# Gate and up as 2x2 block products, with seven products for three of eight pairs of k tiles

## The chip, the cores and the metric

One NeuronCore of a Trainium2 chip runs the whole program. The metric is device time in microseconds, lower is better: 2230.7 us is the median of three runs of the kernel before (2228.87 to 2231.47).

## What is computed

The reference is an encoder of two layers on 256 tokens of width 2048, all in float32. Layer 0 mixes tokens by neighbourhood attention and a gated recurrence, layer 1 by pooling and grouped-query attention. After each mixer every layer does the same:

```
x = layer_norm(ALPHA * x + mixer(x), g1, b1)
f = (silu(x @ w_gate) * (x @ w_up)) @ w_down      # 2048 -> 5632 -> 2048
x = layer_norm(ALPHA * x + f, g2, b2)
```

## The kernel before

All matrix products are made from float32 values that are split in two: `hi`, the value rounded to the matmul's format (fp32r), and `lo`, the remainder. One product of a 128x128 tile of x with a 128x512 tile of weights is three matmuls of 512 columns into one PSUM bank (`mm3`, line 243): x lo by w hi, x hi by w hi, x hi by w lo. x lies transposed in `xT`, as hi and lo, 16 k tiles for each of the two token tiles (`tok`) of 128.

Weights come from HBM in halves: `load_half` (line 140 issues the load on SyncE's queue) brings 128 x 1024 elements, 512 KB, which are two k tiles by 512 columns, into one of four `raw` buffers. ScalarE rounds them into `whi` (line 103) and VectorE subtracts to make `wlo` (line 104). `whi` and `wlo` rotate through a ring of slots, and a slot is rounded into again when TensorE has used it up. Each half feeds 12 matmuls.

The feed-forward part, `ffn`, walks 11 chunks of 512 hidden columns in three phases (`PHASES`: 3, 4 and 4 chunks). A chunk is 8 halves of gate into two banks, Silu on ScalarE (line 367), 8 halves of up into two more, the product of the two on VectorE (line 374), four transposes for each token tile (line 100, TensorE with the identity) and the split into `yT`. After the chunks of a phase come the products with w_down (`in_down`), four column blocks of 512, whose results are added to the residual `res` (lines 257 and 259). At the last block of the last phase the halves are all loaded first and the tokens go one after the other (`tok_major`), so that the layer norm of token tile 0 runs beside the products of tile 1. `out_proj`, which stands ahead of `ffn`, is built in the same way. PSUM's eight banks are three for `acc`, two for `tr` (transposes) and three for `mx`.

The order of instructions on each engine is made when the program is built: a scheduler runs a model of the engines and takes what is ready by priority, which `tc.high_priority` raises. On the chip each engine follows its own fixed order, and semaphores hold an instruction until its inputs are there. So an engine that waits holds up all that stands behind it in its order.

Of the kernel before, what the change touches and what calls it, by code (L numbers as in the profile page):

```python
# [11 lines left out]
F32 = mybir.dt.float32  # L12
F32R = mybir.dt.float32r
# [5 lines left out]
P = 128  # L19
# [4 lines left out]
NCH = 512  # L24
# [45 lines left out]


@with_exitstack
def trunk(ctx: ExitStack, tc: tile.TileContext, a, out):
# [7 lines left out]
    ps = ctx.enter_context(tc.tile_pool(name="ps", bufs=1, space=PSUM))  # L81
# [8 lines left out]
    def acc():  # L90
        return ps.tile([P, NCH], F32, tag="acc", name="acc", bufs=3)

    def trp():
        return ps.tile([P, NCH], F32, tag="tr", name="tr", bufs=2)

    def mxp():
        return ps.tile([P, NCH], F32, tag="mx", name="mx", bufs=3)
# [12 lines left out]
    rings = [(wp, 6)]  # L110
# [38 lines left out]

    def mm_chunk(halves, lhs, outs, tok_major=False, after=None, before=None):  # L150
# [8 lines left out]
        def mms(i, tok, pin=False):  # L159
            hi, lo = loaded[i]  # L160
            k0 = halves[i][1]
            for kk in range(2):
                xh, xl = lhs(tok, k0 + kk)
# [171 lines left out]
    def out_proj(w, order, groups, res, gb):  # L335
        evac, norm = residual_tools(res, *gb)
        lhs = y_lhs(groups)
        xT = new_xT()
        for n in range(4):
            outs = [acc() for _ in range(NT)]  # L340
            halves = [(w[n, 2 * g + i], 4 * g + 2 * i) for g in order for i in range(2)]
# [11 lines left out]
    def ffn(fp, layer, xT, res, gb, last):  # L353
        evac, norm = residual_tools(res, *gb)
        lhs = x_lhs(xT)
        new = None if last else new_xT
        nxt = [None]
        for pi, chunks in enumerate(PHASES):
            groups = {}
            for c in chunks:  # L360
                first = pi == 0 and c == 0
                gouts = [acc() for _ in range(NT)]
                sil = {}

                def silu(tok):
                    sil[tok] = fp.tile([P, NCH], F32, tag="sil", name="sil", bufs=3)
                    nc.scalar.activation(sil[tok], gouts[tok], AF.Silu)

                mm_chunk([(a[f"gate{layer}"][c, i], 2 * i) for i in range(8)], lhs, gouts, tok_major=first, after=silu)
                uouts = [acc() for _ in range(NT)]  # L370
                groups[c] = new_yT()

                def gated(tok):
                    nc.vector.tensor_tensor(sil[tok], sil[tok], uouts[tok], op=mult)
                    s = slice(tok * P, (tok + 1) * P)
                    transpose4(sil[tok], groups[c][0][:, :, s], groups[c][1][:, :, s])

                mm_chunk([(a[f"up{layer}"][c, i], 2 * i) for i in range(8)], lhs, uouts, after=gated)
            end = pi == len(PHASES) - 1
            if end and not last:  # L380
                nxt[0] = new_xT()
            gl = [groups[c] for c in chunks]
            for n in range(4):
                outs = [acc() for _ in range(NT)]
                halves = [(a[f"down{layer}"][n, 2 * c + i], 4 * ci + 2 * i) for ci, c in enumerate(chunks) for i in range(2)]

                def after(tok):
                    with tc.high_priority(offset=1000 if end and n == 3 else 0):
                        evac(tok, n, outs[tok], pi == 0, end)
                        if end and n == 3:  # L390
                            norm(tok, nxt[0], out if last else None)

                mm_chunk(halves, y_lhs(gl), outs, tok_major=(end and n == 3), after=after)
        return nxt[0]
# [29 lines left out]
    def ab_mixer(mp, xT, yT):  # L424
# [239 lines left out]
        for c, ((kind, i), _) in enumerate(ab_plan()):  # L664
            outs = [acc() for _ in range(NT)]
            mm_chunk([(a["ab_in"][c, n], 2 * n) for n in range(8)], lhs, outs, before=load_x if c == 0 else None)
# [5 lines left out]
    def cd_mixer(mp, xT, yT):  # L672
# [118 lines left out]
        for c, (kind, _) in enumerate(cd_plan()):  # L791
            outs = [acc() for _ in range(NT)]
            mm_chunk([(a["cd_in"][c, n], 2 * n) for n in range(8)], lhs, outs, tok_major=(c == 0))
# [10 lines left out]
    with tc.tile_pool(name="ab", bufs=1) as mp:  # L804
        ab_mixer(mp, xT, yT)
# [4 lines left out]
    open_ring(ctx.enter_context(tc.tile_pool(name="wx", bufs=1)), 2)  # L810
    with tc.tile_pool(name="f0", bufs=1) as fp:
        open_ring(fp, 3)
        xT = out_proj(a["ab_out"], AB_OUT_GROUPS, yT, res, load_gb(fp, 0, "mix"))
        xT = ffn(fp, 0, xT, res, load_gb(fp, 0, "ffn"), False)
    rings.pop()
    yT = [new_yT() for _ in range(4)]
    with tc.tile_pool(name="cd", bufs=1) as mp:
        cd_mixer(mp, xT, yT)
    with tc.tile_pool(name="f1", bufs=1) as fp:
        open_ring(fp, 3)  # L820
        xT = out_proj(a["cd_out"], CD_OUT_GROUPS, yT, res, load_gb(fp, 1, "mix"))
        ffn(fp, 1, xT, res, load_gb(fp, 1, "ffn"), True)
# [54 lines left out]

def layout(i):
# [26 lines left out]
    for l in range(2):  # L905
        m[f"gate{l}"] = pieces(f["ffn_w_gate"][l])
        m[f"up{l}"] = pieces(f["ffn_w_up"][l])
# [24 lines left out]
```

## Time and profile before

| | |
|---|---|
| median of 3 runs | 2230.7 us |
| profiled execution | 2229.76 us |
| its span, first to last instruction | 2228.0 us |
| TensorE busy | 2201.6 us, 10180 instructions |
| VectorE busy | 1313.6 us, 1662 instructions |
| ScalarE busy | 994.5 us, 1258 instructions |
| loads | 416.78 MB from HBM, 188 GB/s over the span |
| granted TensorE clock | 0.996 of full speed |

Times are microseconds. PE is TensorE, DVE VectorE, ACT ScalarE, SP SyncE. A matmul's busy time overlaps the next one's, so the distance between starts tells its cost, not its duration. A row of a group gives the number of instructions, their busy time and the mean in ns; what follows is the idle time before them and what ended it.

### The profile page before, as it was taken

How to read it: one execution, taken by the hardware profiler on the slowest of the kernel's cores; microseconds unless marked ns; L12 is line 12 of the kernel's file. 1: busy time of each engine (PE TensorE's matmuls, PEld its weight loads, DVE VectorE, ACT ScalarE, POOL GpSimd, SP SyncE). 2: the span in 40 equal slices, each digit the busy share in tenths (PEclk: the TensorE clock that was granted, in tenths of full speed). 3: DMA queues.
4: the chain of work that ended last, by engine and by line, in shares of the span. 5: the costliest groups of instructions: out<-in, count | busy, mean ns of one | idle time of the engine just before them, and what ended most of it. 6: DMA issues, size and time to landing. Idle time of an engine off the chain costs nothing.

```text
span 2228.0 us, 26810 instructions
## 1 busy us (share of the span) xinstructions
PE 2201.6 (99%) x10180; PEld 1833.9 (82%) x10180; DVE 1313.6 (59%) x1662; ACT 994.5 (45%) x1258; POOL 83.1 (4%) x67
## 2 busy tenths in 40 slices
PE   8999999999999999999999999999999999999997
PEld 7888888887888888888888788878888888888886
DVE  6886688667555545554455676665554554544454
ACT  6445544546443444344443564444444444444431
POOL 0010001002000000000000200020000000000001
PEclk9999999999999999999999999999999999999999
DMA  8555545676655556565656464656555555656562
GB/s 293 161 161 180 173 130 183 219 250 211 205 187 191 190 188 194 184 199 184 197 176 199 151 207 141 235 171 227 188 190 192 186 192 186 198 179 201 183 197 71
DMA packets 118898, 420.66 MB, mean 189 GB/s; under 512 B 14448, under 2 KB 17008, under 8 KB 117488
## 3 DMA queue, kind: packets, MB, share of 16 engines
q1 hardware_dynamic: 118768, 418.94, 57.4%
q8 instruction: 80, 1.31, 0.2%
q14 instruction: 50, 0.41, 0.1%
HBM read 416.78 MB, written 2.10 MB: 188 GB/s over the span
## 4 chain that ended last, share of the span: by engine, by line
PE 96%; DVE 2%; ACT 1%; DMA 0%; issue 0%; POOL 0%; DVEq 0%; ACTq 0%; POOLq 0%
PE acc L243 91%; PE tr L100 2%; PE mx L530 1%; PE mx L243 1%; DVE wlo L104 1%; DVE xTl L319 0%; PE mx L576 0%; PE mx L783 0%; ACT whi L103 0%; ACT res L288 0%; DVE res L274 0%; DMA raw<-in_cd_in 0%; DMA x<-in_xT 0%; DVE res L278 0%; PE mx L766 0%
## 5 line engine op out<-in xcount | busy, mean ns | idle before, releaser
L104 DVE TENSOR_TENSOR wlo<-raw,whi 128x1024 fp32r<-128x1024 f32 (+1 forms) x761 | 938.4, 1236 | 726.2 <-ACT whi L103 708.8
L103 ACT CAST whi<-raw 128x1024 fp32r<-128x1024 f32 (+1 forms) x761 | 800.6, 1053 | 987.4 <-PE acc L243 836.2
L243 PE MATMUL acc<-whi,xTl 128*128 128x512 f32 x2080 | 814.7, 394 | 13.7 <-DVE xTl L319 8.0
L243 PE MATMUL acc<-whi,xTh 128*128 128x512 f32 x2080 | 814.4, 392 | 0.0
L243 PE MATMUL acc<-wlo,xTh 128*128 128x512 f32 x2080 | 808.7, 391 | 0.3 <-DVE wlo L104 0.3
L243 PEld LDWEIGHTS acc<-whi,xTl 128*128 128x128 f32 x2080 | 392.3, 189 | 93.5 <-DVE xTl L319 8.5
L243 PEld LDWEIGHTS acc<-wlo,xTh 128*128 128x128 f32 x2080 | 392.0, 188 | 81.6 <-DVE wlo L104 0.7
L243 PEld LDWEIGHTS acc<-whi,xTh 128*128 128x128 f32 x2080 | 392.4, 189 | 78.5
L243 PE MATMUL acc<-whi,yTl 128*128 128x512 f32 x960 | 375.0, 391 | 0.1
L243 PE MATMUL acc<-whi,yTh 128*128 128x512 f32 x960 | 373.8, 389 | 0.0
L243 PE MATMUL acc<-wlo,yTh 128*128 128x512 f32 x960 | 370.0, 389 | 0.0
L243 PEld LDWEIGHTS acc<-wlo,yTh 128*128 128x128 f32 x960 | 180.2, 188 | 37.8 <-DVE wlo L104 0.4
L243 PEld LDWEIGHTS acc<-whi,yTl 128*128 128x128 f32 x960 | 180.3, 188 | 37.0 <-DVE yTl L789 0.3
L243 PEld LDWEIGHTS acc<-whi,yTh 128*128 128x128 f32 x960 | 180.3, 188 | 36.7
L200 POOL TENSOR_TENSOR rstd<-rstd,mhalf 128x4 f32<-128x4 f32 (+2 forms) x18 | 17.6, 976 | 1799.8 <-DVE rstd L197 1656.9
L104 DVE TENSOR_TENSOR yTl<-tr,yTh 128x512 fp32r<-128x512 f32 x48 | 31.1, 686 | 79.5 <-ACT yTh L103 79.5
L103 ACT CAST yTh<-tr 128x512 fp32r<-128x512 f32 x48 | 26.0, 589 | 94.4 <-PE tr L100 94.3
L320 POOL TENSOR_TENSOR res<-res,bet 128x512 f32<-128x512 f32 x24 | 39.4, 1650 | 26.0 <-PE tr L100 14.6
L259 DVE TENSOR_TENSOR res<-res,acc 128x512 f32<-128x512 f32 x32 | 21.9, 685 | 25.4 <-PE acc L243 24.9
L530 PEld LDWEIGHTS mx<-qq,kk 128*128 128x128 f32 x256 | 33.6, 191 | 2.6
L530 PE MATMUL mx<-qq,kk 128*128 128x128 f32 x256 | 33.8, 274 | 0.0
L257 DVE SCALAR_TENSOR_TENSOR res<-res,acc 128x512 f32<-128x512 f32 x32 | 21.8, 683 | 16.7 <-PE acc L243 15.7
(162 smaller groups left out, 829.4 us busy)
## 6 DMA issues: line engine op xcount, KB each, us to landing
raw<-in_gate SPq DMA_DIRECT2D x176, 512.0 KB, 3.9
raw<-in_up SPq DMA_DIRECT2D x176, 512.0 KB, 4.3
raw<-in_down SPq DMA_DIRECT2D x176, 512.0 KB, 4.1
raw<-in_ab_in SPq DMA_DIRECT2D x127, 512.0 KB, 4.1
raw<-in_cd_in SPq DMA_DIRECT2D x40, 512.0 KB, 4.3
raw<-in_ab_out SPq DMA_DIRECT2D x32, 512.0 KB, 4.7
raw<-in_cd_out SPq DMA_DIRECT2D x32, 512.0 KB, 4.0
x<-in_xT SPq DMA_DIRECT2D x8, 256.0 KB, 6.3
```

What stands on the lines that cost most here:

```text
L100: return nc.tensor.transpose(o, src, eye)
L103: nc.scalar.copy(hi, src)
L104: nc.vector.tensor_tensor(lo, src, hi.bitcast(F32), op=sub)
L200: nc.gpsimd.tensor_tensor(r[:, :n], r[:, :n], mhalf[:, :n], op=ALU.pow)
L243: ins = nc.tensor.matmul(o, lhs[a], rhs[b], start=start and n == 0, stop=stop and n == 2)
L257: nc.vector.scalar_tensor_tensor(r, r, ALPHA, psum, op0=mult, op1=add)
L259: nc.vector.tensor_tensor(r, r, psum, op=add)
L320: nc.gpsimd.tensor_tensor(r, r, bet[:, s], op=add)
L530: nc.tensor.matmul(m[:, 2 * h + s, :], kk[:, h, s * P : (s + 1) * P], qq[:, h, r * P : (r + 1) * P], start=True, stop=True,)
```

## The change

A pair of k tiles (k1, k2) with the two token tiles, and gate and up as two columns, is a 2x2 by 2x2 block product: eight products of 128x128 by 128x512. `unit` does a chunk as eight pairs in the order of `PAIRS`. Five pairs are plain: their eight products go to four banks, c11 and c21 (gate of token tile 1 and 2), c12 and c22 (up). The pairs in `SEVEN` (5, 6 and 7) take seven products in the manner of Strassen and Winograd: three with weights as they are, four with sums of weights. `load_seven` loads the four blocks of a pair at once, 1 MB into the single buffer `rs`, makes four sums `z` on VectorE and splits the three plain blocks and the four sums into `sh` and `sl` (two buffers each). `forms_of` makes, once per layer, the four sums of x blocks for the three pairs (`fs`, split into `fm`); its buffer `xs` has the tag of `rs`, and `fs` that of `z`. Four of the seven products have banks of their own (p1, p6, p5, p7), which `unit` combines with c11 to c22 at the end of a chunk.

A unit so takes all eight banks: `open_banks("sides")` lays PSUM out as two sides of four, a unit's c banks on one and its p banks on the other, and the sides swap. Chunk 0 stays as it was (`whole`), as do the down products. The ring of weight slots is 4 during units (6 to 11 before), with 7 more around out_proj and around the last phase's down product. Gate and up lie together in HBM as `gu`, with up's two k tiles swapped. The diff, cut:

```diff
@@ -68,6 +68,9 @@
+PAIRS = (0, 1, 5, 2, 3, 6, 4, 7)
+SEVEN = (5, 6, 7)
...
@@ -78,7 +81,23 @@
-    ps = ctx.enter_context(tc.tile_pool(name="ps", bufs=1, space=PSUM))
+    banks = {}
+    def open_banks(kind):
+        if banks:
+            banks["stack"].close()
+        stack = ctx.enter_context(ExitStack())
+        pool = stack.enter_context(tc.tile_pool(name="ps", bufs=1, space=PSUM, reuse_waits="tile"))
+        banks.update(stack=stack, pool=pool, kind=kind, side=0)
+    def bank(tag, bufs):
+        return banks["pool"].tile([P, NCH], F32, tag=tag, name=tag, bufs=bufs)
+    def side_bank(other=False):
+        return bank("ab"[banks["side"] ^ other] + "side", 4)
...
@@ -88,13 +107,13 @@
     def acc():
-        return ps.tile([P, NCH], F32, tag="acc", name="acc", bufs=3)
+        return bank("acc", 3) if banks["kind"] == "uses" else side_bank()
     def trp():
-        return ps.tile([P, NCH], F32, tag="tr", name="tr", bufs=2)
+        return bank("tr", 2) if banks["kind"] == "uses" else side_bank(True)
...
@@ -107,7 +126,7 @@
-    rings = [(wp, 6)]
...
@@ -350,48 +371,160 @@
+    def forms_of(sp, xT):
+        n = len(SEVEN)
+        k = [slice(2 * SEVEN[0] + e, 2 * SEVEN[0] + 2 * n, 2) for e in range(2)]
+        xs = sp.tile([P, NT, 2 * n, P], F32, tag="rs", name="xs", bufs=1)
+        for t in range(NT):
+            s = slice(2 * SEVEN[0], 2 * SEVEN[0] + 2 * n)
+            nc.vector.tensor_tensor(xs[:, t], xT[0][t][:, s, :].bitcast(F32), xT[1][t][:, s, :].bitcast(F32), op=add)
+        x11, x12, x21, x22 = (xs[:, t, e : 2 * n : 2, :] for t in range(2) for e in range(2))
+        fs = sp.tile([P, 4, n, P], F32, tag="z", name="fs", bufs=1)
+        e, f, g, h = (fs[:, i] for i in range(4))
+        nc.vector.tensor_tensor(e, x22, x21, op=sub)
+        nc.vector.tensor_tensor(f, e, x11, op=add)
+        nc.vector.tensor_tensor(g, x11, x21, op=sub)
+        nc.vector.tensor_tensor(h, x12, f, op=sub)
+        hi, lo = split_tile(sp, [P, 4, n, P], fs, "fm")
+        out = []
+        for i in range(n):
+            k1, k2 = 2 * SEVEN[i], 2 * SEVEN[i] + 1
+            x = lambda t, k: (xT[0][t][:, k, :], xT[1][t][:, k, :])
+            e, f, g, h = (at((hi, lo), slice(None), j, i) for j in range(4))
+            out.append({"11": x(0, k1), "12": x(0, k2), "22": x(1, k2), "e": e, "f": f, "g": g, "h": h})
+        return dict(zip(SEVEN, out))
+    def load_seven(sp, src):
+        with tc.high_priority(offset=400):
+            raw = sp.tile([P, 4, NCH], F32, tag="rs", name="rs", bufs=1)
+            hi = sp.tile([P, 7, NCH], F32R, tag="sh", name="sh", bufs=2)
+            lo = sp.tile([P, 7, NCH], F32R, tag="sl", name="sl", bufs=2)
+            z = sp.tile([P, 4, NCH], F32, tag="z", name="z", bufs=1)
+            last_load[0] = nc.sync.dma_start(raw, src).ins
+            nc.scalar.copy(hi[:, :3], raw[:, :3])
+            nc.vector.tensor_tensor(z[:, :2], raw[:, 0:3:2], raw[:, 3:4].to_broadcast([P, 2, NCH]), op=add)
+            nc.vector.tensor_tensor(z[:, 2], z[:, 0], raw[:, 2], op=add)
+            nc.vector.tensor_tensor(z[:, 3], z[:, 2], raw[:, 1], op=add)
+            nc.vector.tensor_tensor(lo[:, :3], raw[:, :3], hi[:, :3].bitcast(F32), op=sub)
+            split(hi[:, 3:], lo[:, 3:], z)
+        return lambda i: (hi[:, i, :], lo[:, i, :])
+    SEVEN_ORDER = ((0, "11", "p1"), (5, "f", "p6"), (3, "e", "p5"), (4, "g", "p7"), (1, "12", "c11"), (2, "h", "c12"), (6, "22", "c21"))
+    def unit(sp, w, lhs, forms, yT):
+        b = {n: side_bank() for n in ("c11", "c21", "c12", "c22")}
+        begun = set()
+        def product(name, x, wt, last):
+            mm3(b[name], x, wt, name not in begun, last)
+            begun.add(name)
+        sevens = [p for p in PAIRS if p in SEVEN]
+        plain = [p for p in PAIRS if p not in SEVEN]
+        for p in PAIRS:
+            if p in SEVEN:
+                if p == sevens[0]:
+                    b.update((n, side_bank(True)) for n in ("p1", "p6", "p5", "p7"))
+                wt = load_seven(sp, w[p])
+                for i, x, name in SEVEN_ORDER:
+                    product(name, forms[p][x], wt(i), p == sevens[-1])
+            else:
+                for n, ks in ((0, (2 * p, 2 * p + 1)), (1, (2 * p + 1, 2 * p))):
+                    hi, lo = load_half(w[p][:, 2 * n : 2 * n + 2])
+                    for tok in range(NT):
+                        for kk in range(2):
+                            name = f"c{tok + 1}{n + 1}"
+                            product(name, lhs(tok, ks[kk]), (hi[:, kk, :], lo[:, kk, :]), name == "c22" and p == plain[-1] and kk == 1)
+        with tc.high_priority(offset=1000):
+            g0, w_, v, x = (sp.tile([P, NCH], F32, tag=n, name=n, bufs=1) for n in ("g0", "g1", "u0", "u1"))
+            nc.scalar.copy(g0, b["p1"])
+            nc.vector.tensor_tensor(w_, g0, b["p6"], op=sub)
+            nc.vector.tensor_tensor(v, w_, b["p5"], op=add)
+            nc.vector.tensor_tensor(w_, w_, b["p7"], op=add)
+            nc.vector.tensor_tensor(x, w_, b["p5"], op=add)
+            nc.vector.tensor_tensor(g0, g0, b["c11"], op=add)
+            nc.scalar.activation(g0, g0, AF.Silu)
+            nc.vector.tensor_tensor(v, b["c12"], v, op=sub)
+            nc.vector.tensor_tensor(w_, w_, b["c21"], op=add)
+            nc.scalar.activation(w_, w_, AF.Silu)
+            nc.vector.tensor_tensor(x, b["c22"], x, op=sub)
+            banks["side"] ^= 1
...
+        groups = {0: whole(0, mix_pool, True)}
+        close_mix()
+        stack = ExitStack()
+        sp = later_pool(stack, f"s{layer}")
+        open_banks("sides")
+        with tc.high_priority(offset=2000):
+            forms = forms_of(sp, xT)
...
+                if c not in groups:
+                    groups[c] = new_yT()
+                    unit(sp, w[c], lhs, forms, groups[c])
...
+            if end:
+                stack.close()
+                open_banks("uses")
+                open_ring(later_pool(stack, f"er{layer}"), 7)
+                fp = later_pool(stack, f"e{layer}")
+                gb = load_gb(fp, layer, "ffn")
+                nxt = None if last else new_xT()
+                evac, norm = residual_tools(res, *gb)
+            else:
+                evac, _ = residual_tools(res, None, None, None)
...
+            if not end:
+                banks["side"] ^= 1
...
@@ -801,25 +934,40 @@
-    with tc.tile_pool(name="ab", bufs=1) as mp:
-        ab_mixer(mp, xT, yT)
+    with tc.tile_pool(name="wab", bufs=1) as wab:
+        rings.append((wab, 2))
+        with tc.tile_pool(name="ab", bufs=1) as mp:
+            ab_mixer(mp, xT, yT)
+    rings.pop()
...
-    open_ring(ctx.enter_context(tc.tile_pool(name="wx", bufs=1)), 2)
-    with tc.tile_pool(name="f0", bufs=1) as fp:
-        open_ring(fp, 3)
...
+    def layer_end(i, w, groups, yT, last):
+        stack = ExitStack()
+        open_ring(later_pool(stack, f"fr{i}"), 7)
+        fp = later_pool(stack, f"f{i}")
+        def close():
+            rings.pop()
+            stack.close()
+        xT = out_proj(w, groups, yT, res, load_gb(fp, i, "mix"))
+        return ffn(i, xT, res, fp, close, last)
+    xT = layer_end(0, a["ab_out"], AB_OUT_GROUPS, yT, False)
+    yT = [new_yT() for _ in range(4)]
+    with tc.tile_pool(name="wcd", bufs=1, reuse_waits="tile") as wcd:
+        rings.append((wcd, 4))
+        with tc.tile_pool(name="cd", bufs=1, reuse_waits="tile") as mp:
+            cd_mixer(mp, xT, yT)
     rings.pop()
...
@@ -873,6 +1021,12 @@
+def pairs(gate, up):
+    g, u = (w.reshape(KT // 2, 2, P, w.shape[1] // NCH, NCH).transpose(3, 0, 2, 1, 4) for w in (gate, up))
+    return np.ascontiguousarray(np.concatenate([g, u[:, :, :, ::-1]], axis=3))
```

Two places of the order, as the scheduler made it. VectorE between chunk 0 and chunk 1 of layer 0, before (`sil` is the product of gate and up, `yTl` the remainder of its transpose):

```order
L104 TENSOR_TENSOR wlo<-raw,whi 128x1024 x15
L374 TENSOR_TENSOR sil<-sil,acc 128x512 x2
L104 TENSOR_TENSOR wlo<-raw,whi 128x1024
L104 TENSOR_TENSOR yTl<-tr,yTh 128x4x128 x2
L104 TENSOR_TENSOR wlo<-raw,whi 128x1024 x15
```

And now, between chunk 0 and unit 1:

```order
L123 TENSOR_TENSOR wlo<-raw,whi 128x1024 x9
L480 TENSOR_TENSOR sil<-sil,acc 128x512 x2
L381 TENSOR_TENSOR xs<-xTh_3814,xTl_3816 128x768
L381 TENSOR_TENSOR xs<-xTh_3815,xTl_3817 128x768
L123 TENSOR_TENSOR yTl<-tr,yTh 128x4x128 x2
L385 TENSOR_TENSOR fs<-xs 128x384
L387 TENSOR_TENSOR fs<-xs 128x384
L386 TENSOR_TENSOR fs<-fs,xs 128x384
L388 TENSOR_TENSOR fs<-xs,fs 128x384
L123 TENSOR_TENSOR fml<-fs,fmh 128x1536
L407 TENSOR_TENSOR z<-rs 128x1024
L123 TENSOR_TENSOR wlo<-raw,whi 128x1024
```

The sums of x stand behind the products of chunk 0's gate and up, and the first load into `rs` (line 407 reads it) needs `xs` to be done with. Four of the nine `wlo` in the first row belong to unit 1.

TensorE at the end of the last phase of layer 0, where the chunks end and the down product begins (`ident` marks transposes, yT numbers tell the chunk), before:

```order
L243 MATMUL acc_9058<-wlo_9098,yTh_8264 128x512
L243 MATMUL acc_9058<-whi_9115,yTl_8265 128x512
L243 MATMUL acc_9058<-whi_9115,yTh_8264 128x512
L100 MATMUL tr_9039<-ident_72,sil_8886 128x128 x4
L100 MATMUL tr_9047<-ident_72,sil_8888 128x128 x4
L243 MATMUL acc_9059<-whi_9061,yTl_7951 128x512
L243 MATMUL acc_9059<-whi_9061,yTh_7950 128x512
```

And now (`bside` are banks of the unit, `sh` and `sl` its weights):

```order
L264 MATMUL bside_8818<-sh_9072,xTl1_3817 128x512
L264 MATMUL bside_8818<-sh_9072,xTh1_3815 128x512
L264 MATMUL bside_8818<-sl_9073,xTh1_3815 128x512
L119 MATMUL bside_9120<-ident_72,g0_9104 128x128 x4
L119 MATMUL bside_9128<-ident_72,g1_9105 128x128 x4
L264 MATMUL acc_9158<-whi_9161,yTl_7856 128x512
L264 MATMUL acc_9158<-whi_9161,yTh_7855 128x512
```

The transposes stood among the down matmuls of earlier chunks; they now stand directly behind the last matmul of the unit whose result they transpose, with all down matmuls behind them.

## Rows read from the trace of the kernel before

**Rows 1.** The page's part 1: busy time, share of the span, instructions.

```profile
PE 2201.6 (99%) x10180; PEld 1833.9 (82%) x10180; DVE 1313.6 (59%) x1662; ACT 994.5 (45%) x1258; POOL 83.1 (4%) x67
```

**Rows 2.** The chain of waits, 760 to 905 us: start, length, what.

```profile
767.06 43.55 PE acc L243 x192
810.61 0.87 PE tr L100 x8
811.48 43.57 PE acc L243 x192
```

**Rows 3.** Busy time of each engine in the window of one chunk.

```profile
core 0: us, PE busy (x) PEld busy (x) DVE busy (x) ACT busy (x) POOL busy (x), PEclk, DMA share, GB/s
767.06:811.48 44.42, 44.42 (x202) 36.88 (x201) 22.18 (x20) 19.05 (x21) 0.00 (x0) 1.00 0.58 190
```

**Rows 4.** Waits of TensorE: total us, times, longest.

```profile
PE acc L243 <- DVE xTl L319: 8.0, 2, 4.0
PE acc L243 <- DVE xTl L104: 5.7, 1, 5.7
PE tr L100 <- ACT res L288: 1.0, 1, 1.0
PE acc L243 <- DVE wlo L104: 0.3, 1, 0.3
```

**Rows 5.** Groups by line and shape, VectorE: count, busy us, mean ns.

```profile
L104 DVE TENSOR_TENSOR wlo<-raw,whi 128x1024 fp32r<-128x1024 f32 x759 | 937.0, 1238 | 725.8 <-ACT whi L103 708.5 <-PE acc L243 0.4
L104 DVE TENSOR_TENSOR yTl<-tr,yTh 128x512 fp32r<-128x512 f32 x48 | 31.1, 686 | 79.5 <-ACT yTh L103 79.5
L374 DVE TENSOR_TENSOR sil<-sil,acc 128x512 f32<-128x512 f32 x44 | 30.1, 684 | 0.8
...
L278 DVE SCALAR_TENSOR_TENSOR res<-res,rstd,bet 128x512 f32<-128x512 f32 x6 | 6.4, 1087 | 0.1
```

**Rows 6.** The same for ScalarE.

```profile
L103 ACT CAST whi<-raw 128x1024 fp32r<-128x1024 f32 x759 | 799.3, 1054 | 987.0 <-PE acc L243 836.2 <-issue 65.8 <-DMA raw<-in_ab_out 17.7
...
L103 ACT CAST yTh<-tr 128x512 fp32r<-128x512 f32 x48 | 26.0, 589 | 94.4 <-PE tr L100 94.3
```

**Rows 7.** Timeline of VectorE, two places: start, length, what.

```profile
60.28 1.23 DVE L104 TENSOR_TENSOR wlo<-raw,whi 128x1024 fp32r<-128x1024 f32 x1
61.42 0.42 DVE L547 TENSOR_TENSOR qq<-q,Pf 128x256 f32<-128x256 f32 x1
...
657.56 1.29 DVE L104 TENSOR_TENSOR yTl<-tr,yTh 128x512 fp32r<-128x512 f32 x2 [3.51 <-ACT yTh L103]
```

**Rows 8.** Timeline of VectorE: an instruction and one that reads its result.

```profile
514.53 0.26 DVE L265 BATCH_NORM_AGGREGATE mv<-st 128x2 f32<-128x24 f32 x1
514.82 0.15 DVE L197 TENSOR_SCALAR rstd<-mv 128x1 f32<-128x1 f32 x1
```

**Rows 9.** Loads of 1 MB: count, KB each, median us to landing.

```profile
res<-in_x SPq DMA_DIRECT2D x2, 1024.0 KB, 8.6
...
gam<-in_ln_ffn_g SPq DMA_DIRECT2D x2, 1024.0 KB, 5.8
```

**Rows 10.** Timeline of TensorE behind the last chunk of layer 0.

```profile
1164.06 1.04 PE L100 MATMUL tr<-ident,sil 128*128 128x128 f32 x8
1164.86 0.47 PE L243 MATMUL acc<-whi,yTl 128*128 128x512 f32 x1
```

More of the change, by code (lines that the diff above doesn't have):

```diff
@@ L107, in trunk @@
     pending = []
-    rings = [(wp, 6)]
+    rings = [(wp, 4)]
     turn = [0]
@@ L148, in load_half, with two @@
         return hi, lo
+    def two(k):
+        return k, k + 1
     def mm_chunk(halves, lhs, outs, tok_major=False, after=None, before=None):
@@ L340, in out_proj @@
             outs = [acc() for _ in range(NT)]
-            halves = [(w[n, 2 * g + i], 4 * g + 2 * i) for g in order for i in range(2)]
+            halves = [(w[n, 2 * g + i], two(4 * g + 2 * i)) for g in order for i in range(2)]
             def after(tok):
@@ new lines, in ffn, with whole, silu, gated @@
+    def ffn(layer, xT, res, mix_pool, close_mix, last):
+        lhs = x_lhs(xT)
+        w = a[f"gu{layer}"]
+        def whole(c, pool, first):
+            gouts = [acc() for _ in range(NT)]
+            sil = {}
+            def silu(tok):
+                sil[tok] = pool.tile([P, NCH], F32, tag="sil", name="sil", bufs=3)
+                nc.scalar.activation(sil[tok], gouts[tok], AF.Silu)
+            mm_chunk([(w[c, i][:, :2], (2 * i, 2 * i + 1)) for i in range(8)], lhs, gouts, tok_major=first, after=silu)
+            uouts = [acc() for _ in range(NT)]
+            y = new_yT()
+            def gated(tok):
+                nc.vector.tensor_tensor(sil[tok], sil[tok], uouts[tok], op=mult)
+                s = slice(tok * P, (tok + 1) * P)
+                transpose4(sil[tok], y[0][:, :, s], y[1][:, :, s])
+            mm_chunk([(w[c, i][:, 2:], (2 * i + 1, 2 * i)) for i in range(8)], lhs, uouts, after=gated)
+            return y
+        groups = {0: whole(0, mix_pool, True)}
[5 more added lines that the diff above has]
+            forms = forms_of(sp, xT)
+        nxt = None
@@ L358, in ffn @@
         for pi, chunks in enumerate(PHASES):
-            groups = {}
+            end = pi == len(PHASES) - 1
             for c in chunks:
[L361 to L378, printed above, removed]
@@ L379, in ffn @@
-            end = pi == len(PHASES) - 1
-            if end and not last:
-                nxt[0] = new_xT()
-            gl = [groups[c] for c in chunks]
+                if c not in groups:
+                    groups[c] = new_yT()
+                    unit(sp, w[c], lhs, forms, groups[c])
+            gl = [groups[c] for c in chunks]
+            if end:
+                stack.close()
+                open_banks("uses")
+                open_ring(later_pool(stack, f"er{layer}"), 7)
[5 more added lines that the diff above has]
+                evac, _ = residual_tools(res, None, None, None)
@@ L383, in ffn @@
             for n in range(4):
                 outs = [acc() for _ in range(NT)]
-                halves = [(a[f"down{layer}"][n, 2 * c + i], 4 * ci + 2 * i) for ci, c in enumerate(chunks) for i in range(2)]
+                halves = [(a[f"down{layer}"][n, 2 * c + i], two(4 * ci + 2 * i)) for ci, c in enumerate(chunks) for i in range(2)]
                 def after(tok):
@@ L665, in ab_mixer @@
             outs = [acc() for _ in range(NT)]
-            mm_chunk([(a["ab_in"][c, n], 2 * n) for n in range(8)], lhs, outs, before=load_x if c == 0 else None)
+            mm_chunk([(a["ab_in"][c, n], two(2 * n)) for n in range(8)], lhs, outs, before=load_x if c == 0 else None)
             if c == 0:
@@ L792, in cd_mixer @@
             outs = [acc() for _ in range(NT)]
-            mm_chunk([(a["cd_in"][c, n], 2 * n) for n in range(8)], lhs, outs, tok_major=(c == 0))
+            mm_chunk([(a["cd_in"][c, n], two(2 * n)) for n in range(8)], lhs, outs, tok_major=(c == 0))
             if kind == "kv":
@@ L905, in layout @@
     for l in range(2):
-        m[f"gate{l}"] = pieces(f["ffn_w_gate"][l])
-        m[f"up{l}"] = pieces(f["ffn_w_up"][l])
+        m[f"gu{l}"] = pairs(f["ffn_w_gate"][l], f["ffn_w_up"][l])
         m[f"down{l}"] = pieces(f["ffn_w_down"][l])
```

31 lines of the change are left out of this document (13 added, 18 removed).

## The prediction, made before the run

> **What bounds the kernel now.** I read the shares of the page first [rows 1]: TensorE is busy for 2201.6 of 2228.0 us, VectorE for 1313.6, ScalarE for 994.5. A busy matmul overlaps the next one, so the rate has to come from the chain of waits [rows 2]: 192 matmuls of 512 columns take 43.55 us, 0.2268 us each, and eight transposes between two chunks take 0.87 us. A chunk of gate and up therefore lasts 44.42 us, and the window over one chunk shows the same period, with VectorE at 22.18 us, ScalarE at 19.05 and 190 GB/s of loads inside it at full clock [rows 3]. TensorE's own waits come to about 15 us in the whole run [rows 4]. So the kernel is as long as its matmuls, and half of VectorE is free in these chunks. The time changes by the matmuls taken out, less whatever new idle time appears on TensorE.
>
> **What the change removes.** A pair of k tiles needs 8 block products (2 token tiles x 2 k tiles x gate and up) of 3 matmuls each; a pair in SEVEN needs 7. Three pairs x 10 chunks x 2 layers x 3 matmuls = 180 fewer matmuls of 512 columns: 180 x 0.2268 = 40.8 us. A unit is 183 x 0.2268 + 0.87 = 42.4 us instead of 44.4. The transposes stay.
>
> **What it adds on VectorE and ScalarE.** For VectorE I take start to start rather than duration. Two 512-element instructions in a row end 1.29 us after the first starts, with 0.686 each, so the second starts 0.604 later; a 1024-element one is followed after 1.14 us (60.28 to 61.42) [rows 5, 7]. The slope is (1.14 - 0.604)/512 = 1.047 ns per element, which gives 0.47 us for 384 elements, 0.87 for 768, 1.68 for 1536 and 2.21 for 2048. An instruction that reads the result of the one just before starts 0.03 us after that one's full duration (514.53, 0.26 long, next at 514.82) [rows 8], which for 512 elements costs 0.686 + 0.03 - 0.604 = 0.11 us more. A seven-pair costs 1.14 + 2 x 0.604 + 1.68 + 2.21 = 6.24 us on VectorE, where its two halves cost 2.28. A unit has 10 plain halves (11.4), three seven-pairs (18.7), ten combining instructions (6.0) and two splits of yT (1.2): 37.3 us, plus about ten dependent steps, 1.1 us: 38.4 of 42.4. ScalarE goes by its slope [rows 6], (1.054 - 0.589)/512: 10 x 1.05 + 3 x (1.52 + 1.98) + 5 x 0.59 = 24 us. Loads move the same bytes in 42.4 us, 199 GB/s. The broadcast operand of line 407 (the first sums, into z) is a form that these rows do not show. I take the plain price, since the 512-element forms from SBUF and from PSUM alike stand at 0.684 to 0.686; the bounds are that price and the 1.087 us of the six slow 512-element instructions of line 278 [rows 5], a factor of 1.6, which on one instruction of 1.14 us in three loads is 2.1 us a unit and still under the cover named below.
>
> The Trainium skill, "VectorE: DVE Perf Modes", section "The DRAIN you can't avoid", speaks against this sum: it says that the next VectorE instruction does not begin until the pipe has emptied, and adds that one which is not held may begin earlier. Rows 7 show the earlier start, so here the trace agrees with the exception; by the rule itself a unit would be the sum of durations (6.74 for a seven-pair), 10 x 1.238 + 3 x 6.74 + 10 x 0.684 + 1.4 = 40.8 us, still under 42.4 but with hardly room for a wait.
>
> **Steady units.** Line numbers from here on are those of the changed kernel: 407 to 409 make the four sums z, 410 the remainders of the three plain weights, 445 to 454 combine the banks, 458 multiplies gate by up. I walked the order of VectorE from the combining of one unit to that of the next. It stands four plain halves and the first load of the next unit ahead of the combining, so TensorE has 48 x 0.2268 = 10.9 us of matmuls while VectorE works through about 11 us; the banks of p6, p7 and p5 come free between 0.9 and 9 us after the unit's end, and the matmuls on them stand at 3.4, 7.7 and 13 us. I cost the steady units at nothing. The cover is 4 us of VectorE per unit; if it is gone, each us costs 20 us in all (rivals).
>
> **Where TensorE will newly idle.** Each time counts from the last matmul before the seam.
> First, chunk 0 to unit 1. VectorE does two gate products, two 768-sums, two splits and four 384-sums: 0.7 + 1.74 + 1.2 + 1.9 + 0.2 = 5.7 us. Only then can the first seven-pair be loaded, since its buffer is the one xs was in. 1 MB lands after 5.8 us in one row (gam) and 8.6 in another (res) [rows 9]; I take 5.8, because the halves issued before it have landed by then, so at 11.5. TensorE has 1.2 us of transposes and 48 matmuls, until 12.1. The rounded parts come at 11.5 + 1.52 = 13.0, six matmuls use them until 14.4, and the first remainders need z, one half, one sum and line 410: 11.5 + 1.14 + 1.14 + 0.6 + 1.7 = 16.1. Idle 0.9 + 1.7. The third seven-pair of this unit comes another 0.9 late: 3.5 us.
> Second, unit 1 to 2: VectorE enters it with two halves, a sum and line 410 still before the combining, reaches line 445 at 4.7 us and frees p6's bank at 5.3, where TensorE has done 15 matmuls by 3.4 and waits for line 410 as well: 2.4 us with both waits.
> Third, the end of phase 0: the second token's product of gate and up comes at 13.3 us behind seven combining steps, a split of 2.21, a sum, line 410 and two halves, TensorE stands at its transpose at 12.3, and then waits 1.2 for the next half: 2.3 us. Phase 1 ends with less in the way: 0.5 us.
> Fourth, the end of phase 2. Before, the transposes stand among the down matmuls that need nothing of the last chunk, and all eight follow in 1.04 us without a wait (1164.06) [rows 10]. Now both stand directly behind the unit's last matmul. The chain after that: line 451 ends at 0.55, 448 at 1.2, 458 at 1.9, 452 at 2.45, 454 at 3.05, Silu in between, 458 for the second token at 3.9; the second transposes end at 4.4 where 0.9 was needed: 3.5 us.
> Together 3.5 + 2.4 + 2.3 + 0.5 + 3.5 = 12.2 us a layer, 24.4 us in all. The sum could be 7.0 (only the fourth, which no order of loads can hide) or, with 8.6 us landings in the first two, about 35.
> The rings ahead of out_proj now start with 4 slots instead of 6, 10.9 us of matmuls; a half needs about 2.3 us of ScalarE and VectorE after its slot is free, so I cost this at nothing, with one missed half, 2.7 us, as the bound per layer.
>
> **Sum.** The profiled execution took 2229.76 us, 1.8 over its span, and the median is 2230.7. 2229.76 - 40.8 + 24.4 = 2213.4; against the median 2214.
>
> **Rivals.**
> Hidden seams: the loads land early and only the fourth seam is paid: 2230.7 - 40.8 + 7.0 = 2197 (2190 with none). For it: TensorE waits only 15 us in the kernel before [rows 4], with an order made in the same way. Against it: VectorE has half of its time free there and 4 us of 42 now.
> VectorE becomes the bound: after the third sum ScalarE must round the four sums (1.98 us) before VectorE may subtract, and VectorE waits in place. Three such waits of 2.1 us on 38.4 give 44.7 us a unit, over the 44.4 of before, which is the point from which the change loses: 20 x (44.7 - 42.4) = 46 us more, 2260. For it: the waiting subtraction has every later half queued behind it, and TensorE waits for those. Against it: the order mostly puts two halves between, and the rounding fits under them. (By the DRAIN rule of the Trainium skill's page above, the unit would be 40.8 + 6.3 = 47.1 us, and the time 2214 + 20 x 4.7 = 2308; rows 7 speak against it.)
> One load buffer of 1 MB is too few: if it lands at 8.6 us in every unit, VectorE waits some 2.8 us for one load of the three, uses up its cover, and TensorE loses around 0.7 us in each of 18 units besides 5 at the seams: 2214 + 18 = 2232, no change that could be told.
>
> **How the numbers follow.** Forecast (2204 to 2226) 0.56; hidden seams (below 2204) 0.20; one buffer (2226 to 2236) 0.14; VectorE as bound (above 2236) 0.10. A difference under 0.2%, 4.5 us, cannot be told from none. Faster 0.56 + 0.20 + 0.02 of the third = 0.78, same 0.12, slower 0.10. Range: half of the hidden seams and all of VectorE as bound are left out, 2197 to 2232.
>
> **What would show it.** Right: 8940 matmuls of 512 columns, a steady unit of 42.4 us, VectorE at 37 to 41 us in it; TensorE's waits at about 40 us in all, mostly for lines 123, 410 and 458, with a wait of about 3.5 us at the two last units. Wrong: units above 43 us with waits for the split of the sums (VectorE as bound), or for L407's load; or no waits at the seams. The forecast falls if 1.14 us per 1024 elements does not hold for lines 407 to 410.

## The result, and the profile after

The changed kernel takes 2237.3 us (median of 7 runs, 2234.4 to 2241.7), the kernel before 2230.7: ratio 1.003, 95% interval 1.0018 to 1.0042. It is slower by 0.3%, where 2214 and a range of 2197 to 2232 were predicted.

The page's part 1 of the kernel after, beside [rows 1]: 180 fewer matmuls, as counted, and VectorE up from 1313.6 to 1636.4 us.

```profile
PE 2183.4 (98%) x10000; PEld 1806.8 (81%) x10000; DVE 1636.4 (73%) x2016; ACT 1073.3 (48%) x1280; POOL 80.4 (4%) x67
```

TensorE's waits after, beside [rows 4]. The two entries for xTl are as before, and nearly all else is new:

```profile
PE acc L264 <- DVE xTl L340: 8.0, 2, 4.0
PE bside L119 <- DVE g L458: 6.5, 5, 1.8
PE acc L264 <- DVE xTl L123: 5.6, 1, 5.6
PE aside L264 <- DVE wlo L123: 4.5, 2, 3.4
PE acc L264 <- DVE wlo L123: 3.9, 6, 1.4
...
```

Windows after, beside [rows 3]: 40 us of steady units, then three stretches at seams, and one with what follows it.

```profile
core 0: us, PE busy (x) PEld busy (x) DVE busy (x) ACT busy (x) POOL busy (x), PEclk, DMA share, GB/s
1110.00:1150.00 40.00, 40.00 (x182) 33.11 (x181) 35.35 (x36) 20.34 (x19) 0.00 (x0) 1.00 0.54 179
610.80:620.00 9.20, 7.44 (x18) 5.34 (x19) 9.20 (x11) 4.46 (x5) 0.00 (x0) 0.63 0.37 140
...
669.20:678.00 8.80, 7.54 (x21) 5.55 (x22) 7.44 (x9) 4.81 (x5) 0.00 (x0) 0.61 0.81 254
678.00:688.00 10.00, 10.00 (x45) 8.26 (x44) 8.55 (x10) 3.41 (x4) 0.00 (x0) 1.00 0.60 214
...
1648.30:1654.50 6.20, 6.20 (x17) 4.93 (x18) 4.71 (x6) 2.81 (x3) 0.00 (x0) 0.53 0.91 300
```

The column PEclk is the reading: in the steady units TensorE is never idle and the clock is full. From 1648.3 TensorE is also busy throughout, yet does 17 instructions in 6.2 us where 10 us at full clock hold 45 (from 678.0). It runs at 0.53, near the lower of its two levels (1.2 of 2.4 GHz), and a matmul takes 0.43 us instead of 0.2268. A look at idle time alone misses this: the engine counts as busy.

Where the time went, by landmarks of TensorE in the two profiled executions (spans 2228.0 and 2235.5 us):

| stretch | before | after | change | predicted |
|---|---|---|---|---|
| start to chunk 0 of layer 0 | 528.6 | 528.0 | -0.6 | 0 |
| layer 0, chunk 0 to last unit | 630.7 | 627.6 | -3.1 | -11.7 |
| from there to the layer norm's first transpose | 84.1 | 89.0 | +4.9 | +3.5 |
| border: to the first matmul behind those transposes | 20.3 | 29.7 | +9.3 | 0 |
| second mixer and out_proj | 233.0 | 234.6 | +1.6 | 0 |
| layer 1, chunk 0 to last unit | 631.6 | 621.7 | -9.9 | -11.7 |
| from there to the end | 99.6 | 105.0 | +5.4 | +3.5 |

Counted from the starts in TensorE's timeline: a wait is a step from one start to the next that is over 0.4 us longer than the matmul takes at full clock (0.2268 us for 512 columns, 0.109 for a transpose). The waits rose from 9.9 to 39.3 us. Other matmuls of 512 columns with steps above 0.25 us, at half clock or held up briefly, cost 34.7 us over 0.2268 instead of 18.2, and the remaining short delays rose by 2.4. With the matmuls removed, -40.8 + 29.4 + 16.5 + 2.4 = +7.5, as the span has it.

### The profile page after: what moved, and what is told of

Read it like the earlier page. It is cut to its first block, busy times and chain, and to the rows that moved or that the text cites. A ratio compares the mean times of both kernels' runs of the same rounds, so it can differ in the third digit from the quotient of the medians.

```text
span 2235.5 us, 26590 instructions
## 1 busy us (share of the span) xinstructions
PE 2183.4 (98%) x10000; PEld 1806.8 (81%) x10000; DVE 1636.4 (73%) x2016; ACT 1073.3 (48%) x1280; POOL 80.4 (4%) x67
## 4 chain that ended last, share of the span: by engine, by line
PE 89%; DVE 6%; DMA 2%; issue 2%; ACT 1%; SPq 0%; POOL 0%; DVEq 0%; ACTq 0%; POOLq 0%
PE acc L264 39%; PE bside L264 25%; PE aside L264 21%; DVE wlo L123 2%; DMA rs<-in_gu 2%; PE mx L663 1%; PE mx L264 1%; PE tr L119 1%; DVE sl L410 1%; ACT whi L122 0%; PE aside L119 0%; PE bside L119 0%; DVE xTl L340 0%; ACT sh L406 0%; PE mx L709 0%
## 5 line engine op out<-in xcount | busy, mean ns | idle before, releaser
L264 PE MATMUL acc<-whi,xTl 128*128 128x512 f32 x800 | 319.4, 400 | 14.4 <-DVE xTl L340 8.0
L264 PE MATMUL acc<-wlo,xTh 128*128 128x512 f32 x800 | 315.2, 396 | 5.1 <-DVE wlo L123 3.9
L264 PE MATMUL acc<-whi,xTh 128*128 128x512 f32 x800 | 317.1, 396 | 0.0
L264 PE MATMUL acc<-whi,yTl 128*128 128x512 f32 x512 | 201.3, 394 | 0.1
L264 PE MATMUL acc<-whi,yTh 128*128 128x512 f32 x512 | 200.7, 392 | 0.0
L264 PE MATMUL acc<-wlo,yTh 128*128 128x512 f32 x512 | 198.6, 391 | 0.0
L264 PEld LDWEIGHTS acc<-whi,xTl 128*128 128x128 f32 x800 | 152.4, 190 | 46.0 <-DVE xTl L340 8.5
L264 PEld LDWEIGHTS acc<-wlo,xTh 128*128 128x128 f32 x800 | 151.9, 190 | 39.0 <-DVE wlo L123 6.8
L264 PEld LDWEIGHTS acc<-whi,xTh 128*128 128x128 f32 x800 | 152.5, 191 | 29.1
L264 PE MATMUL bside<-whi,xTl 128*128 128x512 f32 x400 | 157.2, 394 | 1.4 <-DVE g L445 1.4
L123 DVE TENSOR_TENSOR sl<-z,sh 128x2048 fp32r<-128x2048 f32 x60 | 137.3, 2288 | 20.6 <-ACT sh L122 19.5
L264 PEld LDWEIGHTS acc<-wlo,yTh 128*128 128x128 f32 x512 | 96.8, 189 | 20.7 <-DVE wlo L123 0.5
```

Of the source, the lines that this page charges most:

```text
L123: nc.vector.tensor_tensor(lo, src, hi.bitcast(F32), op=sub)
L264: ins = nc.tensor.matmul(o, lhs[a], rhs[b], start=start and n == 0, stop=stop and n == 2)
```

## Theories and experiments

Theory: the seven products save their 41 us; the idle time at the seams, matmuls at half clock behind it, and a late start of the second mixer's loads eat it up. Rivals: VectorE's added work bounds the units, or the new banks and rings cost everywhere. All experiments edit the changed kernel, but for the one with idle doses.

### No seven products

```diff
-SEVEN = (5, 6, 7)
+SEVEN = ()
...
```

> SEVEN is empty: every unit takes its eight products, while the two sides of banks, the ring of 4, the order of loads and the entry to the next mixer stay as changed. Theory (the seven products save their 41 us, and the structure around them, with its idle times and the half clock that follows them, costs more than that): the matmul count is back at 9120, and the time is well above the kernel before, 2241 to 2252 us, because the entry of the second mixer (9 us) and the ends of phases (about 5 us a layer, half clock included) stay. Rival (VectorE's and ScalarE's work for the seven products is what slows the changed kernel): without it the time falls back to that of before, 2231 within 4 us.

Measured 2245.5 us (1.0048 to 1.0073 of before), in the theory's range. Both layers' units take 631.3 and 631.5 us as before, and the border takes 29.9. So the seven products gain something even as changed, and the border's loss is not theirs.

### The second mixer's ring opened earlier

```diff
-                open_ring(later_pool(stack, f"er{layer}"), 7)
+                if not last:
+                    open_ring(later_pool(keep, "wcd"), 4)
+                open_ring(later_pool(stack, f"er{layer}"), 7 if last else 3)
...
```

> The second mixer's ring of four slots is opened ahead of the last down product of layer 0 and shared by it, so that those slots persist across the border (as they did before); the other ring there is 3 instead of 7. Theory (the mixer's first loads issue late, since their slots lie on memory that the last down product still uses): the stretch from 1245 to 1274 us shrinks by about 9 us, idle 7 us less and half clock 3 us less, and the time is 2228 us. Rival (the border waits for the layer norm's transposes, not for loads): the stretch stays within 2 us, 2237 us.

Measured 2234.8 us (1.0004 to 1.0024), 2.5 below the changed kernel and not 9; the runs of the two overlap. The profiled execution is among its fastest (2229.5 of 2228.5 to 2240.6), and in it the border takes 20.7 us. SyncE's loads for the mixer, from 1225 us on, show why: of before, of after, and of this run, start and time to the last issue.

```profile
1229.82 25.61 SPq L140 DMA_DIRECT2D raw<-in_cd_in  x6
```

```profile
1251.39 10.30 SPq L159 DMA_DIRECT2D raw<-in_cd_in  x4
```

```profile
1228.57 33.61 SPq L159 DMA_DIRECT2D raw<-in_cd_in  x8
```

After, no load is issued between 1225 and 1251 us, and ScalarE waits for them at the border; with the slots there beforehand they go out from 1228.6. The border is mended; why most executions gain less than the profiled one stays open. Their mean granted clock is 0.990 to 0.991, where the two fastest have 0.993.

### Two sides kept to the last down block

```diff
             if end:
                 stack.close()
-                open_banks("uses")
...
             for n in range(4):
+                if end and n == 3:
+                    open_banks("uses")
```

> At the end of a layer PSUM stays laid out in two sides until the last of the four down blocks. Theory (the transposes of the last unit stand directly behind it because the new layout needs all its banks): the two waits of 2.0 and 1.55 us at 1156 and 2131 us go, and the half clock behind them (1.1 and 1.7 us) with them: 10 us less in two layers, 2227 us. Rival (the order there has another cause, or the wait comes back where the layout now changes, at the fourth block): 2237 us within 3.

Measured 2227.2 us (0.9974 to 0.9992), as the theory had it. In the kernel after, the timeline of TensorE at the end of layer 0's last unit is this, to be read beside [rows 10]:

```profile
1155.55 0.39 PE L264 MATMUL bside<-sl,xTh 128*128 128x512 f32 x1
1157.78 0.66 PE L119 MATMUL bside<-ident,g 128*128 128x128 f32 x4 [1.84 <-DVE g L458]
1159.77 1.11 PE L119 MATMUL bside<-ident,g 128*128 128x128 f32 x4 [1.33 <-DVE g L458]
1160.54 0.78 PE L264 MATMUL acc<-whi,yTl 128*128 128x512 f32 x1
1161.11 0.63 PE L264 MATMUL acc<-whi,yTh 128*128 128x512 f32 x1
1161.54 0.63 PE L264 MATMUL acc<-wlo,yTh 128*128 128x512 f32 x1
```

Two waits of 1.84 and 1.33 us, then matmuls 0.43 us apart. In this run the transposes stand among down matmuls and wait for nothing, and the stretches to the transposes and to the end take 84.1 and 100.1 us (84.1 and 99.6 in the kernel before).

```profile
1158.47 0.60 PE L119 MATMUL bside<-ident,g 128*128 128x128 f32 x4
```

### Other buffers for the sums of x

```diff
-        xs = sp.tile([P, NT, 2 * n, P], F32, tag="rs", name="xs", bufs=1)
+        xs = [sp.tile([P, n, P], F32, tag=u, name="x" + u, bufs=1) for u in ("g0", "g1", "u0", "u1")]
...
```

> The sums of x blocks take the four small buffers that are used at the end of a unit only, so the first 1 MB load of a layer need not wait for them. Theory (the seams of chunk 0, unit 1 and unit 2 idle because that load starts late): the idle times at 576, 610, 1547 and 1592 us (6.3 us) and the half clock behind them (about 4 us) go for the greater part: 2229 us. Rival (VectorE's order of work alone holds these seams): 2237 us within 2.

Measured 2250.4 us (1.0078 to 1.0105): 13 us slower, where both expected 2237 or less. The first load of layer 0 is issued at 563.7 us instead of 568.1, but the order behind it came out otherwise. ScalarE's timeline of this run at the end of unit 1 in layer 1:

```profile
1598.82 1.47 ACT L406 CAST sh<-rs 128x1536 fp32r<-128x1536 f32 x1 [4.66 <-DMA rs<-in_gu]
1600.19 0.58 ACT L444 COPY g<-bside 128x512 f32<-128x512 f32 x1
```

The copy that frees a bank for the next unit (line 444) stands behind a rounding that waits for the 1 MB load, and TensorE waits 4.6 us for that copy. So this seam hangs on where the later loads stand in the order, not on the start of the first; the theory of this seam fell.

### Both mended

The edits of the second and third experiment together.

> Two edits together: the sides of banks kept until the last down block of a layer, and the second mixer's ring opened ahead of the last down product. Theory (the two losses are independent: 10 us of waits and half clock at the two layer ends, and 9 us at the border of the layers): the border takes 20.5 us as before instead of 29.7, both last down products take 84 and 100 us as before, and the time is 2218 to 2222 us, faster than both kernels. Rival (what one edit gains is given back as half clock or as a wait elsewhere): 2227 us or more.

Measured 2226.6 us (0.9964 to 0.9985), at the rival's bound and not in the theory's range. The border takes 20.6 us and the end 100.1, but the last down product of layer 0 takes 88.1, not 84: TensorE's timeline has a new wait where the layout now changes, with slow matmuls behind it.

```profile
1219.72 0.39 PE L264 MATMUL aside<-wlo,yTh 128*128 128x512 f32 x1
1222.31 0.76 PE L264 MATMUL acc<-whi,yTl 128*128 128x512 f32 x1 [2.20 <-DVE res L280]
1222.87 0.63 PE L264 MATMUL acc<-whi,yTh 128*128 128x512 f32 x1
```

So the two losses are not independent: 4 us of one gain came back as another wait.

### A plain pair at the end of each unit

```diff
-PAIRS = (0, 1, 5, 2, 3, 6, 4, 7)
+PAIRS = (0, 1, 5, 2, 6, 3, 7, 4)
...
```

> On top of both edits of the run before this one: the pairs of k tiles go in the order 0 1 5 2 6 3 7 4, so that a unit ends with a plain pair and the four banks of their own are combined beside it. Theory (the idle time at the seams comes from the combining and the loads that pile up behind the last pair of seven products): the waits at the first two seams and the two ends of phases, 8 to 9 us a layer in the changed kernel, fall to about 4 and the half clock behind them goes with them: 10 us less than the run with both edits alone. Rival (the spacing of the 1 MB loads is what counts, and here it is 10.2 us twice instead of 15.6 and 10.2, under the 12.8 us that one load's round takes): waits for that load in every unit, some 2 us in each of 20, 40 us more.

Measured 2216.5 us (0.9915 to 0.994), 10.1 below the run before, as the theory had it. The waits between units 1 and 2 of layer 0 are gone. At the end of phase 0 the theory was wrong: in layer 0 the waits of 1.8 and 0.6 us in the run before became 0.6 and 5.3, and layer 1 has one of 5.1:

```profile
PE aside L265 <- DVE wlo L124: 10.4, 2, 5.3
```

VectorE's timeline in it. Between the half at 664.06 and the late one at 667.53, TensorE waits while VectorE works on the next unit's sums (L408; L411 just before) and on the combining:

```profile
662.39 1.75 DVE L411 TENSOR_TENSOR sl<-rs,sh 128x1536 fp32r<-128x1536 f32 x1
664.06 1.21 DVE L124 TENSOR_TENSOR wlo<-raw,whi 128x1024 fp32r<-128x1024 f32 x1
665.20 1.21 DVE L408 TENSOR_TENSOR z<-rs 128x1024 f32<-128x1024 f32 x1
666.33 0.68 DVE L453 TENSOR_TENSOR g<-g,bside 128x512 f32<-128x512 f32 x1
666.93 0.68 DVE L455 TENSOR_TENSOR u<-bside,u 128x512 f32<-128x512 f32 x1
667.53 2.34 DVE L124 TENSOR_TENSOR wlo<-raw,whi 128x1024 fp32r<-128x1024 f32 x2
```

### A plain pair at the end, loads spaced as changed

```diff
+FIRST_PAIRS = (0, 1, 5, 2, 3, 6, 4, 7)
+PAIRS = (0, 5, 1, 2, 6, 3, 7, 4)
...
```

> As the run before, but the first unit of a layer keeps the order 0 1 5 2 3 6 4 7 and the others go 0 5 1 2 6 3 7 4: a plain pair at the end, and the 1 MB loads spaced as in the changed kernel (15.6 and 10.2 us). Theory: no wait for the load inside a unit, and the waits at the ends of phases and of layers fall as there; the first seam stays. 5 to 8 us less than the run with both edits alone. Rival (the first pair of seven now stands 5.4 us behind a unit's start, before the banks of the last unit are free): a wait of 1 to 2 us at every unit's start, 20 to 40 us more.

Measured 2218.2 us (0.9922 to 0.9949): 8.3 below the run with both edits. The spacing of loads that the rivals of both runs spoke of makes no difference that can be told.

### Doses of idle time in the kernel before

```diff
+    HOLD = {1: 0, 3: 2, 5: 4, 8: 8}
...
+                    if c in HOLD and tok == 1:
+                        for _ in range(HOLD[c]):
+                            nc.vector.tensor_scalar(sil[tok], sil[tok], 1.0, None, op0=mult)
```

> The kernel before with idle time put in: in chunks 1 to 6, 8 and 9 TensorE's order is kept as written, so the eight transposes stand directly behind a chunk's last matmul, and the product they wait for is followed by 0, 2, 4 and 8 more VectorE multiplications by one in chunks 1, 3, 5 and 8 (about 0.7 us each). No seven products, rings and banks as before. Theory (after an idle time of some 2 us or more TensorE runs for a while at half its clock, 0.43 us a matmul, and that costs beside the idle time itself): no slow matmuls behind the short waits of about 1 us, 5 to 15 slow ones behind the doses of 4 and 8; idle 33 us plus 8 to 12 us of slow matmuls, 2272 to 2276 us. Rival (the slow matmuls in the changed kernel are late inputs, not the clock, and an idle time costs only itself): none behind any dose, 2264 us.

Measured 2267.8 us (1.0146 to 1.0174), between the two, since the short waits did not come. The stretches decide. TensorE's timeline behind the doses of 2 and of 8:

```profile
766.67 0.63 PE L100 MATMUL tr<-ident,sil 128*128 128x128 f32 x4 [2.09 <-DVE sil L383]
767.06 0.48 PE L248 MATMUL acc<-whi,xTl 128*128 128x512 f32 x1
767.37 0.40 PE L248 MATMUL acc<-whi,xTh 128*128 128x512 f32 x1
...
1089.07 1.08 PE L100 MATMUL tr<-ident,sil 128*128 128x128 f32 x4 [5.33 <-DVE sil L383]
1089.81 0.77 PE L248 MATMUL acc<-whi,xTl 128*128 128x512 f32 x1
1090.38 0.63 PE L248 MATMUL acc<-whi,xTh 128*128 128x512 f32 x1
1090.80 0.63 PE L248 MATMUL acc<-wlo,xTh 128*128 128x512 f32 x1
```

And its windows behind the doses of 2 and 8:

```profile
767.00:773.00 6.00, 6.00 (x29) 5.01 (x28) 2.04 (x3) 2.08 (x3) 0.00 (x0) 1.00 0.30 92
...
1089.80:1094.10 4.30, 4.30 (x13) 3.37 (x12) 0.69 (x1) 0.59 (x1) 0.00 (x0) 0.53 0.00 0
```

A single wait of 2.09 us leaves the clock full. Those of 3.48 and 5.33 us are each followed, in both layers, by 9 or 10 slow matmuls that cost 1.7 to 2.1 us more, with halves long ready (VectorE is nearly idle in that window). The sum of the profiled executions fits: 2228.0 + 24.0 of new waits over 0.4 us + 4.1 of shorter delays + 9.7 of slow matmuls = 2265.8, and the span is 2265.6. So the half clock is the clock, not late inputs.

### No seven products, both mended

> SEVEN is empty, with the kept sides and the shared ring of the run with both edits. Theory (the structure around the seven products, that is the sides of banks and the ring of 4 slots, costs nothing once the two places are mended): 2231 us within 3, the time of the kernel before. Rival (the shorter ring of 4 slots costs in the chunks and the down products too): 2236 us or more.

Here SEVEN is empty on top of both edits. Measured 2234.7 us (1.0007 to 1.0025): 3 us over before, just outside the theory's bound and under the rival's, so the changed structure costs some 3 us. Part of it stands in the second mixer, which takes 234.6 us in the profile of this run as in that of the changed kernel, and 233.0 before. Against this the run of the next experiment, which has the seven products and another order, takes 28.8 us less, of the 40.8 that the removed matmuls are worth.

### The next unit's pairs kept out of the phase ends

```diff
+                if n == 1 and not end:
+                    mark[0] = last_load[0]
...
+                    order.enter_context(tc.issue_after(mark[0]))
```

> On top of the order 0 1 5 2 6 3 7 4 with both edits (2216.5 us): at the ends of phases 0 and 1 the first 1 MB load of the next unit is issued behind the loads of the second down block. Theory (TensorE's wait of 5.3 us at 663 and 5.1 us at 1627 us comes from VectorE working on the next unit's pairs of seven products between the halves of the down product, and half clock follows): both waits go, with 1.7 to 2.4 us of half clock each, some 13 us in all, 2204 us. Rival (VectorE is short there anyway, since it needs 2.3 of the 2.7 us of each half besides the combining; or the next unit's first pair now comes late): 2214 us or more.

Measured 2205.9 us (0.9868 to 0.9895), 10.6 below the run it edits. Both waits at the ends of phase 0 are gone, and layer 0's units take 613.5 us.

> As the run before, with that load behind the loads of the third down block. Theory: the waits at the phase ends go as there; the first pair of seven of the next unit has some 16 us less lead, which may cost a wait of up to 2 us at its start; 2204 to 2210 us. Rival as there: 2214 us or more.

With `n == 2` instead, 2205.2 us (0.9868 to 0.9895), the same. These two are the fastest, 1.2% under before.

### More work for VectorE

Line 407's instruction stands twice.

> The order 0 1 5 2 6 3 7 4 with both edits (2216.5 us), and the first sums of every pair of seven (1024 elements, 1.14 us on VectorE) are made twice: 3.4 us more of VectorE in each of 20 units, no more matmuls. Theory (VectorE has about 4 us to spare in a unit of 41.5 us, so the pace of units does not change, only the first pairs of a layer and the ends of phases grow by about one sum each): 2218 to 2226 us. Rival (VectorE is already the bound of a unit): 68 us more, 2285 us.

Measured 2259.0 us (1.0099 to 1.0132): neither. Two steady units of this run, then the same two of the run it edits, with its phase ends mended:

```profile
791.90:832.80 40.90, 40.90 (x186) 33.88 (x185) 34.32 (x35) 20.90 (x20) 0.00 (x0) 1.00 0.49 169
832.80:876.30 43.50, 43.50 (x197) 36.06 (x196) 39.57 (x39) 21.86 (x20) 0.00 (x0) 1.00 0.58 198
```

```profile
768.60:811.30 42.70, 42.70 (x194) 35.36 (x193) 34.54 (x34) 21.88 (x20) 0.00 (x0) 1.00 0.56 189
811.30:853.00 41.70, 41.70 (x189) 34.57 (x188) 33.96 (x35) 21.72 (x21) 0.00 (x0) 1.00 0.52 180
```

84.4 us and 383 matmuls in both: the added work is hidden there, as predicted. The 42 us more come from TensorE's waits in the first two units of a layer and at the ends of phases, half clock included. That is far more than the added work that falls there (6.8 us in the first two units of a layer). The program's order moved with the edit too, so what the added work alone costs is not shown.

## Why the prediction was wrong

- Matmuls removed: right. 180 fewer, and a steady unit takes 42.4 us in the kernel after (three together 127.3).
- VectorE's durations and pace: right. The groups of VectorE after, beside [rows 5], and its timeline in one unit, beside [rows 7]:

```profile
L123 DVE TENSOR_TENSOR sl<-z,sh 128x2048 fp32r<-128x2048 f32 x60 | 137.3, 2288 | 20.6 <-ACT sh L122 19.5
L410 DVE TENSOR_TENSOR sl<-rs,sh 128x1536 fp32r<-128x1536 f32 x60 | 105.2, 1754 | 40.6 <-ACT sh L406 40.4
L407 DVE TENSOR_TENSOR z<-rs 128x1024 f32<-128x1024 f32 x60 | 73.2, 1220 | 29.2 <-DMA rs<-in_gu 29.0
```

```profile
652.05 1.22 DVE L407 TENSOR_TENSOR z<-rs 128x1024 f32<-128x1024 f32 x1
653.19 1.75 DVE L410 TENSOR_TENSOR sl<-rs,sh 128x1536 fp32r<-128x1536 f32 x1
654.86 1.22 DVE L123 TENSOR_TENSOR wlo<-raw,whi 128x1024 fp32r<-128x1024 f32 x1
...
660.78 2.28 DVE L123 TENSOR_TENSOR sl<-z,sh 128x2048 fp32r<-128x2048 f32 x1
662.99 0.68 DVE L458 TENSOR_TENSOR g<-g,u 128x512 f32<-128x512 f32 x1
```

  Line 407 is followed after 1.14 us, line 410 after 1.67, the large remainder after 2.21: the forecast 1.14, 1.68 and 2.21. The form with the broadcast operand costs the plain price, and VectorE waits for its input 29.0 us in 60 loads; in steady units TensorE shows no wait from it.
- Idle time at the seams: the total was near, 21.6 us against 24.4, in part by luck, since the parts missed both ways. Unit 1 to 2 cost 3.2 and 1.0 us (forecast 2.4), the end of phase 0 3.3 and 3.6 (2.3), chunk 0 to unit 1 1.6 and 1.1 (3.5), the end of phase 1 1.0 and nothing (0.5), the end of phase 2 3.5 in each layer (3.5). The waits in the whole run are 39.3 us, as the sign of "about 40" had it, but 5.9 us of that are new waits at the border, which the sum left out.
- The step that failed is the sum: it charged each seam with the idle time alone. Behind the seams TensorE ran at the lower clock, and its matmuls and transposes there cost some 12 us more: 7.2 in layer 0 and 4.7 in layer 1. The doses show that this is a price of the wait itself. The trace of before had it, behind its own two waits of 4.0 us for xTl [rows 4], and it was not read there. The window behind the second of them, in the kernel before:

```profile
1496.80:1502.00 5.20, 5.20 (x12) 4.09 (x13) 3.78 (x15) 0.00 (x0) 0.00 (x0) 0.50 0.82 303
```

   The Trainium skill, "TensorE: Matmul & The Clock Gate", section "HAM oscillation — how this bites in real kernels", says that waits for data can make TensorE fall back to its slower clock, so that what follows starts slow; the trace agrees, 0.43 us a matmul behind the doses.
- The second failed term is "the rings ahead of out_proj", costed at nothing with a bound of 2.7 us a layer. The ring was missed at a border that the prediction didn't name, the start of the second mixer, at 9.3 us. Why its slots were late (they lie where the last down product's ring was) is a reading of the code; that opening them earlier mends it is shown.
- Together 21.6 of waits at the seams, 11.8 of half clock behind them, 4.7 of shorter delays in the units and down products, 9.3 at the border and 1.0 (1.6 in the second mixer, -0.6 at the start) make 48.4 us against 40.8 saved, which is the +7.5 within 0.1. What each of the short delays waits for was not traced.
- The rivals: hidden seams fell at once. VectorE as the bound fell for the units, yet at the seams VectorE is what TensorE waits for. One 1 MB buffer: VectorE does wait for a load in steady units (2.96 us at 1063.6), but TensorE doesn't wait there, where the rival had priced 0.7 us a unit; at the seam of units 1 and 2 VectorE waits 1.96 us for it at 609.3, just ahead of TensorE's waits.

## What to carry to other kernels

Price a new wait of the matmul engine as the wait and, where waits of several us or several close together come, some 10 matmuls at half clock that may follow it (2 us here); read PEclk in windows behind the waits that the kernel has already. Work added to an engine with slack in the steady state was paid at the seams here, so put the seams' order right first: ending units with a plain pair, keeping the units' two sides of banks through three down blocks, opening the second mixer's ring earlier and holding the next phase's loads back turned +0.3% into -1.2% with the same arithmetic. When a change shortens a shared ring, walk every place that used it, not only the one that the change names.

## What the runs showed of the hardware

Behind a single wait of 2.09 us TensorE went on at full clock, behind 3.48 us it did not, in both layers. Yet in the changed kernel the stretch from 610.8 us has a granted clock of 0.63 behind three waits of 0.79, 1.06 and 0.70 us with only three matmuls between them: several short waits did what one of their size did not.

The length of a wait alone does not decide it. In the run with both edits the clock is at half behind a single wait of 2.20 us (1222.31 above), and in the run with more work for VectorE it is full behind one of 3.22 us. The windows behind the two, and TensorE's row at the second:

```profile
1222.30:1225.50 3.20, 3.19 (x8) 2.52 (x9) 1.88 (x3) 0.48 (x1) 0.00 (x0) 0.50 0.47 164
```

```profile
673.70:680.00 6.30, 6.30 (x28) 5.18 (x29) 6.30 (x9) 3.58 (x4) 0.00 (x0) 1.00 0.28 83
```

```profile
673.69 0.51 PE L265 MATMUL aside<-whi,yTl 128*128 128x512 f32 x1 [3.22 <-DVE g L447]
```

What else decides, these runs don't show. So a wait's half clock is a risk to price, and no rule by its length came out of the runs.
